# A decoder trunk on one core: VectorE takes the low parts of the attention's weights from GpSimd, and a weight transfer changes shape

## The chip, the cores and the metric

The kernel runs on one NeuronCore of a Trainium2 chip. Its time is the device time of one execution in microseconds (us); 662.78 us is the median of three runs (661.78, 662.78 and 668.63). The engines are named as in the profile: PE (matmul), PEld (its weight loads), DVE (VectorE), ACT (ScalarE), POOL (GpSimd) and SP (SyncE, which issues the transfers).

## The reference

The reference is a two-layer decoder trunk in float32 for 256 tokens of width 1024. The parts that matter here:

```
layer A: h += W_out( B * causal_dwconv3( C * V ) ),  [B|C|V] = rms_norm(h) @ W_in
         h += swiglu(rms_norm(h))                    hidden width 2816
shared:  kv = rms_norm(h) @ w_kv                     six sets: compressed K and V, selected K and V, window K and V
         k_cmp, v_cmp = silu(blocks @ w1) @ w2       blocks of 32 tokens, stride 16, w1 is 2048 x 256 for each
layer B: q, gates from rms_norm(h) @ w_qg
         h += (gate0*o_cmp + gate1*o_slc + gate2*o_win) @ w_o     16 heads of 64, 4 KV groups
         h += swiglu(rms_norm(h))
out = rms_norm(h)
```

## The kernel before

Every product is computed to nearly float32 accuracy from numbers of a shorter format. A weight piece of 128 x 1024 float32 comes in over DMA into a "raw" tile; its **high part** is a rounded copy (`hi`), its **low part** is the difference raw minus high (`lo`). Activations are split in the same way, and three products (high x high, high x low, low x high) stand for one. `split_weights` (lines 302 to 327) does this for a piece: transfer (L316 or L318), high part (L320 on POOL or L322 on ACT), low part (L326), whose columns are divided between POOL and DVE. The last argument, `pool`, says how: False gives all columns to DVE, True all to POOL, "both" half to each, "hi" the high part to POOL, "all" high and low part to POOL. For the pieces of the attention stage it comes from `CFG["units"]`, whose other entry names the ring of buffers ("a" or "r") of the parts. `CFG["eng"]` does the same for single operations: for `q00` (first half of the split of Q0, `q_split`) "ap" means high part on ACT, low part on POOL; "pd" means high part on POOL, low part on DVE.

A piece has a name: K (keys and values for compression, selection and window), Q, V, Y (the compression's first weights w1), GP (gates), O (output projection). A raw tile in the attention stage has four buffers, a part three for each ring.

The order of the work is a text, `CFG["plan"]` (lines 216 to 224), read from left to right: "A" and "r" fetch the next piece of one of two streams (`Stream.ahead`), "K2a" or "Y00" multiply with one, "CB" makes the blocks for the compression (`cmp_blocks`, L768 is the low part of its blocks), "KR" finishes keys (`key_rest`, with `keyf` at L847 and the key copies over DMA at L855), "S" computes the scores of a head, and so on. "|4", "|5" and "|6" say which engines keep this order as written; the others, from "|4" on all of them and from "|5" on all but PE, are ordered by the scheduler when the program is built. Each engine then works through its list in that fixed order.

For Y the matrix w1 lies in memory as 128 rows (row = parity of the token in its block x 64 + channel) of 4096 columns. Piece `Y{st}{q}` takes tokens 4q to 4q+3 of each half of the block, so it needs both halves of the rows' columns and both parities. It is fetched in two transfers of 64 rows (L316), one for each half, each row in two stretches of 512 columns:

```
w1 = a["w1"][st].rearrange("(two d) x -> d two x", two=2)
takes[f"Y{st}{q}"] = [w1[:, :, (4 * half + q) * 512:(4 * half + q + 1) * 512] for half in range(2)], 1024
```

`cmp_piece` (L770) multiplies it with the tokens `lp` of the blocks.

Of the kernel before, what the change touches and what calls it, by code (L numbers as in the profile page):

```python
# [24 lines left out]
DH = 64  # L25
# [98 lines left out]
         'm5': 'p',  # L124
         'm6': 'p',
         'm7': 'd',
         'q00': 'ap',
         'q01': 'ad',
         'q10': 'pd',
         'q11': 'ad',  # L130
         'q20': 'pd',
         'q21': 'ad',
# [36 lines left out]
 'qdma': 0,  # L169
 'sq': {'n1': 0, 'n3': 1},  # L170
 'units': {'GP': ('a', False),
           'K0a': ('a', 'all'),
           'K0b': ('a', False),
           'K1a': ('r', False),
           'K1b': ('r', 'both'),
           'K2a': ('a', 'both'),
           'K2b': ('a', False),
           'K4a': ('a', 'both'),
           'K4b': ('r', 'both'),
           'O0a': ('r', False),  # L180
           'O0b': ('r', 'all'),
           'O1a': ('r', 'all'),
# [10 lines left out]
           'O6b': ('a', 'all'),  # L193
           'O7a': ('a', 'both'),
           'O7b': ('r', True),
           'Q0a': ('a', 'both'),
           'Q0b': ('r', 'both'),
           'Q1a': ('a', False),
           'Q1b': ('r', 'both'),
           'Q2a': ('a', False),  # L200
           'Q2b': ('a', True),
           'Q3a': ('a', True),
           'Q3b': ('a', True),
           'V0': ('a', True),
           'V1': ('r', 'both'),
           'V2': ('r', False),
           'V3': ('a', True),
           'Y00': ('a', True),
           'Y01': ('a', 'both'),
           'Y02': ('r', False),  # L210
           'Y03': ('a', False),
           'Y10': ('r', True),
           'Y11': ('a', True),
           'Y12': ('a', 'both'),
           'Y13': ('r', 'both')}}
CFG["plan"] = """
H4 K2a H7 K0a A H5 A A K0b A K1a H2 A H0 B0 H1 |4 A K1b H3 NR H6 A A A I NS CR0 CR1 A CB0 K2b Q0a K4a CB1 A
Q0b K4b A Y00 A A A Y10 R0 B1 Y11 A V0 A M0 Y01 A Y02 V1 Y03 J0 Y12 A r A KR4 KR2 A |5 Y13 J1 t0 GP Q1a t1 ck
# [9 lines left out]
def trunk(ctx: ExitStack, tc: tile.TileContext, a):  # L228
    nc = tc.nc
# [32 lines left out]
    def bank(name, kind="short", hold=False):  # L262

        b = min((b for b in ring[kind] if b not in held.values()), key=used.get)
        touch(b)
        if hold:
            held[name] = b
        return psum.tile([P, 512], F32, tag=f"b{b}", name=name)
# [7 lines left out]
    def f(ap):  # L276
        return ap.bitcast(F32)
# [24 lines left out]
    def split_weights(src, name, cols, ring, pool):  # L302
        if (name[0], ring) in spare:
            w, hi, lo = spare.pop((name[0], ring))
        else:
            if phase["name"] == "attention" or name[0] == "O" or name[:2] == "kv":
                w = wp.tile([P, 1024], F32, tag="raw", name=f"w_{name}", bufs=4)
            else:
                w = phase["pool"].tile([P, 1024], F32, tag="raw", name=f"w_{name}", bufs=12)
            hi, lo = (wp.tile([P, 1024], F32R, tag=ring + hl, name=f"{hl}_{name}", bufs=3) for hl in "hl")  # L310
            if name[0] == "O":
                spare[name[0], ring] = [x[:, cols:] for x in (w, hi, lo)]
            w, hi, lo = (x[:, :cols] for x in (w, hi, lo))
        if isinstance(src, list):
            for r, part in enumerate(src):
                nc.sync.dma_start(out=w[r * DH:(r + 1) * DH].rearrange("p (two x) -> p two x", two=2), in_=part)  # L316
        else:
            nc.sync.dma_start(out=w, in_=src)  # L318
        if pool in ("hi", "all"):
            nc.gpsimd.tensor_copy(hi, w)  # L320
        else:
            nc.scalar.activation(hi, w, AF.Copy)  # L322
        cut = {False: 0, True: cols, "both": cols // 2, "hi": 0, "all": cols}[pool]
        for eng, c0, c1 in ((nc.gpsimd, 0, cut), (nc.vector, cut, cols)):
            if c0 < c1:
                eng.tensor_tensor(out=lo[:, c0:c1], in0=w[:, c0:c1], in1=f(hi[:, c0:c1]), op=ALU.subtract)  # L326
        return hi, lo

    class Stream:
# [3 lines left out]
        def ahead(self, n=3):  # L333
            while len(self.ready) < n:
                u = next(self.todo, None)
                if not u:
                    return
                self.ready.append(split_weights(u[1], u[0], u[2], u[4] if len(u) > 4 else self.ring, u[3]))
# [22 lines left out]
    takes = {}  # L361
# [5 lines left out]
    for q in range(4):  # L367
        for st in range(2):

            w1 = a["w1"][st].rearrange("(two d) x -> d two x", two=2)  # L370
            takes[f"Y{st}{q}"] = [w1[:, :, (4 * half + q) * 512:(4 * half + q + 1) * 512] for half in range(2)], 1024
        takes[f"V{q}"] = a["w_v"][q], 1024
    takes["GP"] = a["w_g"], KC * 48

# [395 lines left out]
    def cmp_piece(st, q):  # L770
        if q == 0:
            py[st] = bank(f"py{st}", hold=True)
        wh, wl = wa.take()
        for i in range(4):

            lp = 4 * q + 2 * (i % 2) + i // 2
            first, last = q == 0 and i == 0, q == 3 and i == 3
            x = xc[st].rearrange("p hl g (n l) -> p l (hl g) n", l=16)[:, lp]
            nc.tensor.matmul(py[st][:, :256], x, wh[:, i * 256:(i + 1) * 256], start=first, stop=False)
            nc.tensor.matmul(py[st][:, :256], x, wl[:, i * 256:(i + 1) * 256], start=False, stop=last)  # L780
# [316 lines left out]
    def hid(st):  # L1097
# [6 lines left out]
          "Q": lambda x: q_piece(int(x[0]), "ab".index(x[1])), "R": lambda x: q_rest(int(x)),  # L1104
          "P": lambda x: q_split(int(x)), "M": lambda x: cmp_second(int(x)),
          "Y": lambda x: cmp_piece(int(x[0]), int(x[1])), "J": lambda x: cmp_hidden(int(x)),
          "V": lambda x: value_piece(int(x)), "N": lambda x: value_rest(), "GP": lambda x: gate_proj(),
          "GR": lambda x: gate_rest(), "B": lambda x: bias(int(x)), "t": lambda x: hid(int(x)),
# [156 lines left out]
```

## Time and profile before

| | |
|---|---|
| median of 3 runs | 662.78 us |
| profiled execution, its own time | 669.47 us |
| span of the profiled execution | 667.6 us |
| PE busy | 628.9 us (94%) |
| DVE busy | 490.3 us (73%) |
| ACT busy | 379.1 us (57%) |
| POOL busy | 326.0 us (49%) |
| mean granted TensorE clock | 0.976 of full speed |

Shares of busy time are averages over stages: the convolution layer and the first feed-forward layer up to about 300 us, then the projections and the attention up to about 470 us, then the second feed-forward layer. The table says which engine has the most work over all of them, not which one is waited for in the stage that the change touches.

### The profile page before, as it was taken

Reading aid. Unit: us, or ns where it says so; the run is one execution under the profiler, and the core shown is the slowest. Engines: PE = TensorE matmul, PEld = TensorE weight load, DVE = VectorE, ACT = ScalarE, POOL = GpSimd, SP = SyncE. Lnnn points to the kernel's source line nnn. Section 1 sums busy time; section 2 is a strip of 40 time slices with the busy share of each in tenths; the row PEclk is TensorE's granted clock in tenths of the full one; section 3 lists DMA queues with packets and bytes.
Section 4 is the critical chain, followed back from the end, with each engine's and each line's share of the span. In section 5 each row is a group of like instructions: output and inputs, shape, how many; then the busy total and the mean of one; then the engine's idle time right before and its main releaser. Section 6 shows DMA issues by size and latency. Waiting matters only on the chain.

```text
span 667.6 us, 11200 instructions
## 1 busy us (share of the span) xinstructions
PE 628.9 (94%) x4094; PEld 573.1 (86%) x4094; DVE 490.3 (73%) x773; ACT 379.1 (57%) x744; POOL 326.0 (49%) x285
## 2 busy tenths in 40 slices
PE   7999999999999999879959979999899999999995
PEld 7999998899999999769949869889788888888884
DVE  5688777866666666769996998787986666666664
ACT  7544457545555544437655758997766554444543
POOL 3163225754444444547564675757845444444422
PEclk9999999999999999989989889999899999999998
DMA  8978672655555550031767520003975555555001
GB/s 299 356 303 256 214 245 83 220 190 189 189 187 187 183 179 23 1 127 54 194 171 233 166 95 2 17 17 130 407 291 182 186 179 180 187 186 188 1 1 63
DMA packets 37383, 109.52 MB, mean 164 GB/s; under 512 B 5712, under 2 KB 8144, under 8 KB 37328
## 3 DMA queue, kind: packets, MB, share of 16 engines
q1 hardware_dynamic: 37184, 108.55, 48.0%
q8 instruction: 32, 0.52, 0.3%
q10 hardware_dynamic: 144, 0.26, 0.1%
q14 instruction: 23, 0.19, 0.1%
HBM read 107.22 MB, written 1.05 MB: 162 GB/s over the span
## 4 chain that ended last, share of the span: by engine, by line
PE 75%; DVE 14%; issue 3%; POOL 3%; ACT 3%; DMA 1%; SPq 0%; POOLq 0%; DVEq 0%; ACTq 0%
PE pgu L654 22%; PE pgu L656 11%; PE acc L397 4%; PE acc L398 4%; PE acc L396 4%; PE acc L716 3%; PE acc L715 3%; PE acc L714 3%; DVE n L451 2%; PE pcv L398 2%; PE pcv L397 2%; PE pcv L396 2%; DVE xc L768 1%; POOL l_d L326 1%; PE po L1051 1%
## 5 line engine op out<-in xcount | busy, mean ns | idle before, releaser
L654 PE MATMUL pgu<-n,h_gu 128*128 128x512 f32 x704 | 250.6, 398 | 4.1 <-DVE n L451 2.5
L656 PE MATMUL pgu<-n,l_gu 128*128 128x256 f32 x704 | 197.3, 281 | 0.4 <-DVE l_gu L326 0.4
L654 PEld LDWEIGHTS pgu<-n,h_gu 128*128 128x128 f32 x704 | 132.7, 189 | 35.1 <-DVE n L451 2.5
L326 DVE TENSOR_TENSOR l_gu<-w_gu,h_gu 128x1024 fp32r<-128x1024 f32 x88 | 117.1, 1332 | 26.5 <-ACT h_gu L322 25.4
L656 PEld LDWEIGHTS pgu<-n,l_gu 128*128 128x128 f32 x704 | 133.4, 190 | 2.2 <-DVE l_gu L326 1.1
L667 POOL TENSOR_TENSOR gu<-gu,n_rbc 128x512 f32<-128x512 f32 x40 | 53.2, 1332 | 166.0 <-DVE gu L663 145.1
L672 DVE TENSOR_TENSOR av<-sg,gu 128x256 f32<-128x256 f32 x44 | 79.5, 1809 | 67.9 <-ACT sg L670 67.9
L326 POOL TENSOR_TENSOR l_d<-w_d,h_d 128x1024 fp32r<-128x1024 f32 x43 | 105.2, 2450 | 7.7 <-ACT h_d L322 7.2
L322 ACT ACTIVATE h_gu<-w_gu 128x1024 fp32r<-128x1024 f32 x88 | 92.7, 1053 | 7.1 <-PE pb L397 3.5
L418 ACT ACTIVATE a_h<-av 128x256 fp32r<-128x256 f32 x44 | 18.3, 417 | 78.9 <-DVE av L672 78.9
L322 ACT ACTIVATE h_d<-w_d 128x1024 fp32r<-128x1024 f32 x44 | 46.8, 1063 | 24.5 <-PE acc L716 20.4
L396 PE MATMUL acc<-a_h,h_d 128*128 128x256 f32 x176 | 50.6, 289 | 5.1 <-ACT a_h L418 5.1
L670 ACT ACTIVATE sg<-gu 128x256 f32<-128x256 f32 x44 | 18.2, 417 | 62.1 <-POOL gu L667 52.5
L397 PE MATMUL acc<-a_l,h_d 128*128 128x256 f32 x176 | 50.8, 289 | 0.7 <-DVE a_l L421 0.7
L398 PE MATMUL acc<-a_h,l_d 128*128 128x256 f32 x176 | 50.5, 287 | 0.0
L326 DVE TENSOR_TENSOR l_in<-w_in,h_in 128x768 fp32r<-128x768 f32 (+1 forms) x33 | 38.8, 1187 | 10.7 <-ACT h_in L322 9.5
L322 ACT ACTIVATE h_in<-w_in 128x768 fp32r<-128x768 f32 (+1 forms) x33 | 27.1, 824 | 29.7 <-PE pb L397 20.5
L396 PEld LDWEIGHTS acc<-a_h,h_d 128*128 128x128 f32 x176 | 34.3, 196 | 6.4 <-ACT a_h L418 5.6
L661 ACT ACTIVATE gu<-pgu 128x256 f32<-128x256 f32 x88 | 32.4, 370 | 11.4 <-PE pgu L656 11.4
L398 PE MATMUL pcv<-n,l_in 128*128 128x256 f32 x128 | 36.9, 288 | 1.7 <-DVE l_in L326 1.7
L396 PE MATMUL pcv<-n,h_in 128*128 128x256 f32 x128 | 36.7, 287 | 1.5 <-ACT h_in L322 1.5
L663 DVE TENSOR_TENSOR gu<-pgu,gu 128x256 f32<-128x256 f32 x88 | 36.4, 416 | 1.4 <-ACT gu L661 1.3
(432 smaller groups left out, 1642.1 us busy)
## 6 DMA issues: line engine op xcount, KB each, us to landing
w_gu<-in_w_gu SPq DMA_DIRECT2D x88, 512.0 KB, 4.1
w_d<-in_w_down SPq DMA_DIRECT2D x44, 512.0 KB, 3.4
w_in<-in_w_in SPq DMA_DIRECT2D x31, 384.0 KB, 6.4
w_wo<-in_w_out SPq DMA_DIRECT2D x8, 512.0 KB, 6.7
w_kvY<-in_w SPq DMA_DIRECT2D x16, 256.0 KB, 4.2
w_kvV<-in_w_v SPq DMA_DIRECT2D x4, 512.0 KB, 3.7
h<-in_xT SPq DMA_DIRECT2D x3, 256.0 KB, 5.9
out<-y SPq DMA_DIRECT2D x3, 256.0 KB, 2.3
```

The costliest lines, as they stand in the source:

```text
L322: nc.scalar.activation(hi, w, AF.Copy)
L326: eng.tensor_tensor(out=lo[:, c0:c1], in0=w[:, c0:c1], in1=f(hi[:, c0:c1]), op=ALU.subtract)
L396: nc.tensor.matmul(out, wh, xh, start=start, stop=False, skip_group_check=True)
L397: nc.tensor.matmul(out, wh, xl, start=False, stop=False, skip_group_check=True)
L398: nc.tensor.matmul(out, wl, xh, start=False, stop=stop, skip_group_check=True)
L654: nc.tensor.matmul(ps[j][c], uh[:, cols], x[:, :, k], start=k == 0, stop=False, skip_group_check=True)
L656: nc.tensor.matmul(ps[j][c][:, :S], ul[:, cols], x[:, 0, k], start=False, stop=k == KC - 1, skip_group_check=True)
L661: nc.scalar.activation(gus[j][:, c], ps[j][c][:, S:], AF.Copy)
L663: nc.vector.tensor_tensor(out=gus[j][:, c], in0=ps[j][c][:, :S], in1=gus[j][:, c], op=ALU.add)
L667: (nc.gpsimd if j < NF - 2 else nc.vector).tensor_tensor(out=gu, in0=gu, in1=norm.bc.unsqueeze(1).to_broadcast([P, 2, S]), op=ALU.mult)
L672: nc.vector.tensor_tensor(out=av, in0=sg, in1=gu[:, 1], op=ALU.mult)
L714: nc.tensor.matmul(out, xh, wh, start=start, stop=False, skip_group_check=True)
```

## The change

The low parts of all K, Q, V and Y pieces go to DVE whole (entries False), K0a's high part goes from POOL to ACT, and the two splits q00 and q10 take ACT for the high and DVE for the low part. The entries of O stay. A Y piece now holds one parity (q % 2) of eight tokens in each half, so that it can be fetched in one transfer of 128 rows of 1024 columns; `cmp_piece` takes the tokens to match.

```
-         'q00': 'ap',
+         'q00': 'ad',
-         'q10': 'pd',
+         'q10': 'ad',
...
-           'K0a': ('a', 'all'),
+           'K0a': ('a', False),
-           'K1b': ('r', 'both'),
-           'K2a': ('a', 'both'),
+           'K1b': ('r', False),
+           'K2a': ('a', False),
-           'K4a': ('a', 'both'),
-           'K4b': ('r', 'both'),
+           'K4a': ('a', False),
+           'K4b': ('r', False),
-           'Q0a': ('a', 'both'),
-           'Q0b': ('r', 'both'),
+           'Q0a': ('a', False),
+           'Q0b': ('r', False),
-           'Q1b': ('r', 'both'),
+           'Q1b': ('r', False),
-           'Q2b': ('a', True),
-           'Q3a': ('a', True),
-           'Q3b': ('a', True),
-           'V0': ('a', True),
-           'V1': ('r', 'both'),
+           'Q2b': ('a', False),
+           'Q3a': ('a', False),
+           'Q3b': ('a', False),
+           'V0': ('a', False),
+           'V1': ('r', False),
-           'V3': ('a', True),
-           'Y00': ('a', True),
-           'Y01': ('a', 'both'),
+           'V3': ('a', False),
+           'Y00': ('a', False),
+           'Y01': ('a', False),
-           'Y10': ('r', True),
-           'Y11': ('a', True),
-           'Y12': ('a', 'both'),
-           'Y13': ('r', 'both')}}
+           'Y10': ('r', False),
+           'Y11': ('a', False),
+           'Y12': ('a', False),
+           'Y13': ('r', False)}}
...
-        if isinstance(src, list):
-            for r, part in enumerate(src):
-                nc.sync.dma_start(out=w[r * DH:(r + 1) * DH].rearrange("p (two x) -> p two x", two=2), in_=part)
-        else:
-            nc.sync.dma_start(out=w, in_=src)
+        nc.sync.dma_start(out=w, in_=src)
...
-            w1 = a["w1"][st].rearrange("(two d) x -> d two x", two=2)
-            takes[f"Y{st}{q}"] = [w1[:, :, (4 * half + q) * 512:(4 * half + q + 1) * 512] for half in range(2)], 1024
+            w1 = a["w1"][st, q % 2 * DH:(q % 2 + 1) * DH].rearrange("d (half x) -> half d x", half=2)
+            takes[f"Y{st}{q}"] = w1[:, :, q // 2 * 1024:(q // 2 + 1) * 1024], 1024
...
-            lp = 4 * q + 2 * (i % 2) + i // 2
+            lp = 8 * (q // 2) + 2 * i + q % 2
```

## Rows read from the trace of the kernel before

**Rows 1.** The page, chain of waits: shares of the span by engine.
```profile
PE 75%; DVE 14%; issue 3%; POOL 3%; ACT 3%; DMA 1%; SPq 0%; POOLq 0%; DVEq 0%; ACTq 0%
```

**Rows 2.** Windows: length, busy PE, PEld, DVE, ACT, POOL; clock, DMA share, GB/s.
```profile
326.00:336.00 10.00, 9.85 (x74) 9.41 (x72) 9.49 (x9) 8.15 (x12) 6.21 (x3) 1.00 0.55 150
336.00:346.00 10.00, 3.04 (x11) 2.09 (x11) 9.91 (x9) 4.52 (x6) 6.71 (x4) 0.96 0.59 158
346.00:362.00 16.00, 15.65 (x72) 15.04 (x73) 10.25 (x15) 8.10 (x13) 5.91 (x5) 0.81 0.94 252
```

**Rows 3.** Timeline of PE: start, duration, line, tiles, shapes, [idle before, releaser].
```profile
346.35 0.56 PE L779 MATMUL py<-h_kvY,xc 128*128 128x256 f32 x1 [3.88 <-DVE keyf L847]
...
361.12 0.39 PE L780 MATMUL py<-l_kvY,xc 128*128 128x256 f32 x1
...
396.94 0.46 PE L964 MATMUL sa<-kh,q 128*128 128x144 f32 x1 [4.89 <-DVE q L421]
```

**Rows 4.** Timeline of DVE: low parts of the compression's blocks.
```profile
327.52 1.34 DVE L768 TENSOR_TENSOR xc<-cf,xc 64x480 fp32r<-64x480 f32 x2
329.18 8.68 DVE L768 TENSOR_TENSOR xc<-cf,xc 64x480 fp32r<-64x480 f32 x4 [0.33 <-ACT xc L767]
```

**Rows 5.** Timeline of POOL, the same stretch.
```profile
332.20 2.42 POOL L326 TENSOR_TENSOR l_kvY<-w_kvY,h_kvY 128x1024 fp32r<-128x1024 f32 x1 [1.06 <-ACT h_kvY L322]
334.56 2.77 POOL L326 TENSOR_TENSOR l_kvV<-w_kvV,h_kvV 128x1024 fp32r<-128x1024 f32 x1
337.30 2.81 POOL L326 TENSOR_TENSOR l_kvY<-w_kvY,h_kvY 128x1024 fp32r<-128x1024 f32 x1
```

**Rows 6.** Line L326: low parts on DVE, ns min/median/max.
```profile
L326 DVE TENSOR_TENSOR l_gu<-w_gu,h_gu x88: 1209/1224/3458, 92.7 to 644.4; 128x1024 fp32r<-128x1024 f32 x88
```

**Rows 7.** Timeline of DVE, 284 to 395 us.
```profile
284.75 2.05 DVE L672 TENSOR_TENSOR av<-sg,gu 128x256 f32<-128x256 f32 x1 [0.48 <-ACT sg L670]
...
293.14 0.42 DVE L672 TENSOR_TENSOR av<-sg,gu 128x256 f32<-128x256 f32 x1 [0.48 <-ACT sg L670]
...
304.62 0.47 DVE L451 SCALAR_TENSOR_TENSOR n<-h,gains,n 128x256 fp32r<-128x256 f32 x1
...
311.97 2.36 DVE L451 SCALAR_TENSOR_TENSOR n<-h,gains,n 128x256 fp32r<-128x256 f32 x1
...
318.69 1.78 DVE L326 TENSOR_TENSOR l_kvK4a<-w_kvK4a,h_kvK4a 128x512 fp32r<-128x512 f32 x1
...
370.25 0.29 DVE L421 TENSOR_TENSOR hv<-sy,hv 128x128 fp32r<-128x128 f32 x1
370.81 2.38 DVE L421 TENSOR_TENSOR hv<-sy,hv 128x128 fp32r<-128x128 f32 x1 [0.26 <-ACT hv L418]
...
385.81 3.43 DVE L326 TENSOR_TENSOR l_O2b<-w_O2b,h_O2b 128x256 fp32r<-128x256 f32 x1
...
392.57 2.17 DVE L998 TENSOR_TENSOR cb<-cb,cm 128x64 f32<-128x64 f32 x1
```

**Rows 8.** Timeline of ACT: an idle stretch, and a wait for a landing.
```profile
284.30 0.42 ACT L670 ACTIVATE sg<-gu 128x256 f32<-128x256 f32 x1 [3.12 <-DVE gu L667]
...
315.61 1.06 ACT L322 ACTIVATE h_kvK4a<-w_kvK4a 128x1024 fp32r<-128x1024 f32 x1 [3.00 <-DMA w_kvK4a<-in_w_kv]
```

**Rows 9.** Line L316, ns min/median/max; timeline of SP's queue.
```profile
L316 SPq DMA_DIRECT2D w_kvY<-in_w x16: 595/600/630, 318.5 to 346.4; - x16
...
318.51 6.80 SPq L316 DMA_DIRECT2D w_kvY<-in_w  x6
```

**Rows 10.** Transfers: count, KB each, median us from issue to landing.
```profile
w_kvV<-in_w_v SPq DMA_DIRECT2D x4, 512.0 KB, 3.7
...
w<-in_w SPq DMA_DIRECT2D x4, 64.0 KB, 2.4
```

**Rows 11.** Windows as rows 2: one transfer alone, and the fullest stretch.
```profile
282.00:288.00 6.00, 6.00 (x49) 5.81 (x48) 5.00 (x6) 1.58 (x4) 4.44 (x3) 1.00 0.25 87
...
470.00:480.00 10.00, 8.59 (x39) 7.25 (x40) 9.79 (x13) 7.36 (x15) 7.75 (x7) 0.83 1.03 413
```

## The prediction

> **What bounds the kernel now.** I read the page first: the chain of waits lies mostly on PE, then on DVE [rows 1]. The change touches only weights used between the tail of the first feed-forward layer (about 280 us) and the first score heads (about 400 us), so I cut that stretch into windows [rows 2]: PE is full from 326 to 336 and nearly full from 346 to 362, but works 3.04 of 10 us from 336 to 346, and DVE is at 9.91 there. In PE's own order [rows 3] the longest of these waits ends at 346.35 (3.88 us); the last compression product is at 361.12; a further 4.89 us of idleness ends at 396.94, on a DVE split of Q. So PE bounds the stage, except where DVE is late.
>
> **Why DVE is late.** Two low-part subtractions of the blocks (L768) take 1.34 us; the next four, of the same shape, take 8.68 [rows 4]. Beside them POOL runs three low parts end to end [rows 5], and each slow DVE subtraction ends with one of these. So a DVE operation with two operands in SBUF stands still while a POOL low part runs. The same pairs recur [rows 7]: `av` 2.05 against 0.42 us, the norm's low part 2.36 against 0.47, `hv` 2.38 against 0.29, l_O2b 3.43 for 256 columns, a 64-column add 2.17, which at its size would need under 0.3.
>
> **The change, part by part.**
>
> *Low parts to DVE.* Nine full and eleven half units move (K0a, Q2b, Q3a, Q3b, V0, V3, Y00, Y10, Y11 full). A full low part costs DVE 1.23 us unblocked [rows 6], POOL 2.42 [rows 5]; a half adds about 0.6. By place, with the unblocked durations of rows 4 and 7:
> - Tail: `av` gets back 1.6, K0a's low part adds 1.2 but can go into DVE's pauses. K0a's high part goes to ACT, 1.06 us like K4a's, and ACT idles 3.12 us there [rows 8]. I take -1 (0 to -1.6).
> - 310 to 326: the norm's low part gets back 1.9; l_kvK4a and its twin l_kvQ0b, 1.78 at half size, become 1.23 whole, 1.1 together; two more norm low parts of this kind about 1 each: 5.0. K1b, Q0a and K4b add 0.55 each. Net -3.3.
> - 329 to 345: the four subtractions get back 8.68 - 4 x 0.67 = 6.0. Four full low parts (4.9), a half (0.6) and Q0's low part (about 0.7) come in: +0.2. w2s and Q's split, which stand right behind them, were held by the last row of rows 5 and by POOL's own part of the split, about 1 each by my estimate: -1.9. With the line above DVE is 5.2 earlier at 346.35, and PE has 7 us of idleness to give it from.
> - 364 to 374: `hv` 2.1 and the like before it 2.1, against V3 and Q2b 2.5: -1.8, of which PE can use 1.
> - 385 to 397: l_O2b about 2.6, the add 1.9, against Q3a and Q3b 2.5: -2 of PE's 4.89.
>
> Sum -9.2 us (-3 to -13: order kept at the far end, half of it lost at the near one). q00 and q10 are in it. POOL's order is free in this stretch or runs ahead; what comes off it hides nothing. SP issues eight transfers instead of sixteen, 0.60 us each [rows 9]: 4.8 us or more of SP's queue; behind them stand only the key copies, which nothing reads before the scores. I cost that at nothing.
>
> *The transfer.* This is the term that decides. Before, every weight transfer has 64 or 128 as outermost dimension on both sides. The new one has `half d x` on the DRAM side: outermost is 2. No row shows what such a transfer takes. Below: like a V piece, 128 rows of 4 KB, 3.7 us [rows 10]. Above: if a transfer is dealt to the DMA engines along its outermost dimension, it runs on two of the sixteen. One busy engine moves 87/(16 x 0.25) = 21.8 GB/s where a transfer runs alone, and 413/(16 x 1.03) = 25.1 where all are full [rows 11]. Half a piece (262 KB) then takes 12.0 or 10.4 us. The nearest row by size says 3.7; by shape none is near, since no row has an outermost dimension below 64. I take the upper case, and 11.2 us in it, because the instruction offers nothing but two parts to share out.
> The Trainium skill, DMA: Bandwidth & Descriptors, section "Why a DMA increments its semaphore by 16 and not by 1", says it outright: the number of engines is the largest up to 16 that divides the size of the slowest dimension on both sides, here 2; by its "Rules for kernel authors" alone, which prefer one transfer of 128 partitions over two halves, the sum would be -9. No row of this case shows either for such a shape.
>
> All eight pieces would use the same two engines, one after another. First issue 318.51 [rows 9], fixed part 2.4 us by the landing of the 64 KB weights [rows 10]: 320.9. Eight x 11.2 = 89.6, and two V pieces' shares on these engines, 2 x 1.4 (32.8 KB at 23.4 GB/s): 413.3. Four raw buffers keep at least one piece queued. Then ACT 1.06, DVE 1.23 and 1.8 of products (8 at 0.22): 417.4, against 361.5: +56. The wait stands in three queues: SP's next piece waits for a raw buffer, with GP, Q1a and the key copies behind it; ACT's high part waits for the landing, with the high parts of Q0 and the keys behind it; DVE's low part waits for ACT, with `keyf` behind it. PE takes its products in a fixed order and waits for all of them, then for GP, Q1a, V2 and the scores. What hides in it: the relief up to 346 is worth nothing more, since DVE waits anyway; the tail's -1 stays, and so do the later -3. PE comes back from thin work at the lower clock, at most +3; I take +1. Net +53.
>
> **Sum.** The profiled execution took 669.47 (span 667.6), 6.7 above the median of 662.78. 669.5 + 53 = 722.5; put on the median, 716.
>
> **The rivals.**
> - *Two engines* (forecast, 0.70): 716; own range 702 to 727 (10.4 to 12.0 us a piece gives -6 and +6; relief and clock -8 to +5). For: the shape. Against: no row.
> - *Sixteen engines, DVE freed* (0.19): Y pieces land like V, and the -9.2 is all there is: 653.6, range 649 to 659. It decides if a piece holds its engines for less than (361.5 - 4.1 - 320.9 - 2.8)/8 = 4.2 us, and up to 4.2 + 9.2/8 = 5.4 us the change is no slower. For: rows 4, 5, 7 leave little doubt of the blocking.
> - *Sixteen engines, the waits move to DVE's queue* (0.11): a low part that POOL used to wait with now waits on DVE for its landing and its high part, in front of L768, the norm and `keyf`. ACT waited 3.00 us for K4a [rows 8]; two such waits take back 6 of 9: 659, range 655 to 670. For: DVE is at 9.91. Against: half of most units was on DVE already.
>
> **Numbers.** 1% (6.6 us) is about what a measurement of this kernel can tell from no change. Faster 0.18 (nearly all of the second case), same 0.09 (most of the third), slower 0.73. The range 652 to 727 holds most of the first case (about 0.62), the third and most of the second.
>
> **What would show it.** Two engines: Y issues landing after 10 us and more each, growing; ACT's high parts of Y spaced by about 11 us; PE waiting on them; the DMA share near 0.13 (2 of 16) between 330 and 410; the last compression product near 415. If instead Y lands at about 4 us, the first case falls. The blocking: L768 about 0.67 each throughout, `hv` 0.3, `av` 0.42 in the tail. If these stay long, something other than the low parts on POOL holds DVE. Wrong in size: if two engines alone move more than 25 GB/s each, or if the pieces are issued well before 318.

## The result, and the profile after

The changed kernel takes 706.2 us (median of 6 runs, 705.79 to 708.52) against 665.59 us for the kernel before on the same chip (6 runs, 661.78 to 669.49): ratio 1.0617 [1.0562, 1.0671], slower. Its profiled execution has a span of 706.7 us against 667.6; the mean granted clock went from 0.976 to 0.941.

The page's chain of waits, shares of the span by engine, has DMA, which held 1% before, level with DVE in second place [rows 1]:

```profile
PE 63%; DMA 13%; DVE 13%; POOL 4%; ACT 3%; issue 3%; SPq 0%; POOLq 0%; ACTq 0%; DVEq 0%
```

The windows that answer to rows 2 (length, busy PE, PEld, DVE, ACT, POOL; clock, DMA share, GB/s):

```profile
326.00:336.00 10.00, 4.42 (x28) 4.02 (x27) 6.36 (x9) 5.65 (x9) 0.00 (x0) 0.84 0.28 94
336.00:346.00 10.00, 0.00 (x0) 0.00 (x0) 0.00 (x0) 0.00 (x0) 0.00 (x0) 0.50 0.13 51
346.00:362.00 16.00, 5.90 (x15) 3.88 (x16) 7.63 (x9) 5.58 (x7) 0.00 (x0) 0.61 0.23 78
```

From 336 to 346 none of the five engines works at all. The DMA share is 0.13, which is 2 of 16, and those two move 51 GB/s, 25.5 each. ACT's timeline (start, duration, line, tiles, [idle before, releaser]) shows what all wait for:

```profile
325.88 1.06 ACT L318 ACTIVATE h_kvY<-w_kvY 128x1024 fp32r<-128x1024 f32 x1 [9.07 <-DMA w_kvY<-in_w]
346.94 1.06 ACT L318 ACTIVATE h_kvY<-w_kvY 128x1024 fp32r<-128x1024 f32 x1 [15.12 <-DMA w_kvY<-in_w]
...
392.51 1.06 ACT L318 ACTIVATE h_kvY<-w_kvY 128x1024 fp32r<-128x1024 f32 x1 [7.58 <-DMA w_kvY<-in_w]
404.14 1.06 ACT L318 ACTIVATE h_kvY<-w_kvY 128x1024 fp32r<-128x1024 f32 x1 [10.57 <-DMA w_kvY<-in_w]
```

The eight high parts of Y stand over (404.14 - 325.88) / 7 = 11.2 us apart on average. PE follows, and its last compression product ends at 408.4 where it ended at 361.5 before [rows 3], 46.9 us later:

```profile
405.25 0.58 PE L774 MATMUL py<-h_kvY,xc 128*128 128x256 f32 x1 [8.44 <-ACT h_kvY L318]
...
408.01 0.43 PE L775 MATMUL py<-l_kvY,xc 128*128 128x256 f32 x1
```

SP's timeline answers to rows 9, and the page's transfers (KB each, us to landing) to rows 10. The first Y issue is 6 us earlier than before, and a V piece that now shares the queue with Y lands after 19.5 us instead of 3.7:

```profile
312.43 9.23 SPq L314 DMA_DIRECT2D w_kvY<-in_w  x3
321.76 4.06 SPq L314 DMA_DIRECT2D w_kvV<-in_w_v  x1
```

```profile
w_kvV<-in_w_v SPq DMA_DIRECT2D x4, 512.0 KB, 19.5
```

DVE is freed where the change takes a low part off POOL. Its timeline, to be read against rows 4 and 7: eight subtractions of the blocks take 0.68 each and end to end, and the `av` that took 2.05 in the tail takes 0.42. The other `av` there, 0.42 before, now takes 2.32, while `l_d`, a low part that the change leaves on POOL (second fence), runs beside it:

```profile
285.08 0.42 DVE L668 TENSOR_TENSOR av<-sg,gu 128x256 f32<-128x256 f32 x1
...
289.88 2.32 DVE L668 TENSOR_TENSOR av<-sg,gu 128x256 f32<-128x256 f32 x1 [0.48 <-ACT sg L666]
...
328.11 5.44 DVE L764 TENSOR_TENSOR xc<-cf,xc 64x480 fp32r<-64x480 f32 x8
...
419.41 0.28 DVE L417 TENSOR_TENSOR hv<-sy,hv 128x128 fp32r<-128x128 f32 x1
```

```profile
289.54 2.38 POOL L322 TENSOR_TENSOR l_d<-w_d,h_d 128x1024 fp32r<-128x1024 f32 x1 [10.97 <-ACT h_d L318]
```

So the change holds two effects of opposite sign. The experiments take them apart, then size each. Each ratio is to runs of the kernel before on the same chip; its median there was 662.25, 663.48 or 662.97. A ratio is turned into us by multiplying with 663. Single executions of the kernel before lie between 661 and 670, and those of `tail_only` and `middle_only` below fall into two groups some 7 us apart, so terms of a few us are given with their intervals.

### The profile page after: what moved, and what is told of

It reads as the page before. It is cut to its first block, busy times and chain, and to the rows that moved or that the text cites. A ratio compares the mean times of both kernels' runs of the same rounds, so it can differ in the third digit from the quotient of the medians.

```text
span 706.7 us, 11153 instructions
## 1 busy us (share of the span) xinstructions
PE 630.7 (89%) x4094; PEld 571.1 (81%) x4094; DVE 476.3 (67%) x783; ACT 380.1 (54%) x746; POOL 286.6 (41%) x262
## 2 busy tenths in 40 slices
DMA packets 36118, 109.51 MB, mean 155 GB/s; under 512 B 5472, under 2 KB 7904, under 8 KB 36064
## 4 chain that ended last, share of the span: by engine, by line
PE 63%; DMA 13%; DVE 13%; POOL 4%; ACT 3%; issue 3%; SPq 0%; POOLq 0%; ACTq 0%; DVEq 0%
PE pgu L650 19%; DMA w_kvY<-in_w 11%; PE pgu L652 10%; PE acc L393 3%; PE acc L394 3%; PE acc L392 3%; PE acc L711 3%; PE acc L712 3%; PE acc L710 3%; PE pcv L394 2%; PE pcv L393 2%; PE pcv L392 2%; DVE n L447 2%; DVE av L668 2%; DVE p L968 1%
## 5 line engine op out<-in xcount | busy, mean ns | idle before, releaser
L322 DVE TENSOR_TENSOR l_kvY<-w_kvY,h_kvY 128x1024 fp32r<-128x1024 f32 x8 | 9.8, 1225 | 63.2 <-ACT h_kvY L318 63.2
L318 ACT ACTIVATE h_kvY<-w_kvY 128x1024 fp32r<-128x1024 f32 x8 | 8.4, 1056 | 68.6 <-DMA w_kvY<-in_w 68.6
L774 PE MATMUL py<-h_kvY,xc 128*128 128x256 f32 x32 | 13.9, 440 | 34.7 <-ACT h_kvY L318 32.2
L774 PEld LDWEIGHTS py<-h_kvY,xc 128*128 128x128 f32 x32 | 9.9, 313 | 36.7 <-ACT h_kvY L318 34.0
## 6 DMA issues: line engine op xcount, KB each, us to landing
w_kvV<-in_w_v SPq DMA_DIRECT2D x4, 512.0 KB, 19.5
```

## The experiments

**The two halves of the change.** `low_parts_only` has the entries of the change and the transfers of before:

```
 CFG of the kernel after
 for r, part in enumerate(src):        # two transfers of 64 rows, as before
     nc.sync.dma_start(out=w[r * DH:(r + 1) * DH]..., in_=part)
```

> One part alone: the low parts, K0a's high part and the two splits of Q as in the changed kernel, the Y pieces still in two transfers of 64 rows. Theory A (two engines: the outermost dimension of 2 confines each Y transfer to two DMA engines, and only that costs time): Y pieces land after about 4 us, the last compression product ends near 352 us, and the relief of DVE is all that is left: 9 us faster than the kernel before (3 to 13), 652 to 662. Theory B (DVE's queue: low parts that POOL used to wait with stand in DVE's queue and hold up the blocks and keys; the transfer is harmless): as slow as the changed kernel, 40 us slower than before.

Measured: 647.54 us, ratio 0.975 [0.9707, 0.9794]. The low parts alone are worth 16.6 us (13.7 to 19.4), more than the 9 (3 to 13) that were expected.

`transfer_only` has the single transfer with the entries of before:

```
 CFG of the kernel before
+nc.sync.dma_start(out=w, in_=src)     # "half d x": outermost 2 in DRAM
```

> The other part alone: Y pieces in one transfer with outermost dimension 2, low parts and splits divided between POOL and DVE as before. Theory A: 45 to 60 us slower than before, Y high parts on ACT 10 to 12 us apart, and some 5 to 9 us slower than the changed kernel, because POOL's low parts still hold up DVE ahead of the first Y transfer and behind the last. Theory B: within 1% of the kernel before.

Measured: 718.66 us, ratio 1.0818 [1.0758, 1.0878], which is +54 us (50 to 58), and 13 above the changed kernel, where 5 to 9 were expected. Its timelines of SP and of ACT, to be held against those of the changed kernel above:

```profile
317.34 9.44 SPq L314 DMA_DIRECT2D w_kvY<-in_w  x3
326.95 3.96 SPq L314 DMA_DIRECT2D w_kvV<-in_w_v  x1
```

```profile
330.96 1.06 ACT L318 ACTIVATE h_kvY<-w_kvY 128x1024 fp32r<-128x1024 f32 x1 [4.55 <-DMA w_kvY<-in_w]
...
408.48 1.06 ACT L318 ACTIVATE h_kvY<-w_kvY 128x1024 fp32r<-128x1024 f32 x1 [11.27 <-DMA w_kvY<-in_w]
```

From the first high part of Y to the last it takes 77.5 us here and 78.3 us in the changed kernel: DVE's relief leaves the length of the stream as it is. But the stream starts 4.9 us earlier in the changed kernel (312.43 against 317.34), since the work ahead of it is relieved, and this start passes whole into the end: the last compression product ends at 413.4 here and at 408.4 there.

**Is it the outermost dimension?** The bytes, the tile and the single transfer stay; only the layout of `w1` in memory changes. In `one_of_128` a piece is 128 rows of 1024 in a row:

```
-            takes[f"Y{st}{q}"] = w1[:, :, q // 2 * 1024:(q // 2 + 1) * 1024], 1024
+            takes[f"Y{st}{q}"] = a["w1"][st, q], 1024
-        "w1": ... x[n].reshape(16, P, 256).transpose(1, 0, 2).reshape(P, 4096)
+        "w1": ... x[n].reshape(2, 2, 4, 2, DH, 256).transpose(1, 3, 0, 4, 2, 5).reshape(4, P, 1024)
```

> The changed kernel with w1 laid out in DRAM so that a Y piece is 128 rows one after the other: still one transfer of 512 KB, same bytes on the chip, same tokens, outermost dimension 128. Theory A: Y lands after about 4 us, 9 us faster than before (3 to 13), and within 2 us of the kernel with the low parts alone: that eight issues replace sixteen is worth nothing. Theory B: 40 us slower than before, like the changed kernel.

Measured: 646.31 us, ratio 0.9732 [0.9689, 0.9775]. It is the fastest kernel of this study, though not to be told from `low_parts_only` on the same chip (645.25 to 647.28 against 646.51 to 649.06).

`outer_4`, `outer_8` and `outer_16` put one row that nobody reads behind every 32, 16 or 8 rows of this layout, so that the rows no longer merge into one dimension and the outermost is 4, 8 or 16:

```
+            takes[f"Y{st}{q}"] = a["w1"][st, q, :, :n], 1024        # n = 32, 16, 8
+        "w1": ... .reshape(4, k, n, 1024)[:, :, [*range(n), 0]]     # k = 4, 8, 16
```

> As the kernel with 128 rows one after the other, but with an unread row behind every 32 in DRAM, so that the outermost dimension is 4. Theory A: four engines, 5.2 to 6 us per piece (131 KB at 21.8 to 25.1 GB/s), eight of them 45 us from the first issue near 312: last compression product near 364 to 370, so about as long as the kernel before (-1% to +1%), and 10 us longer than with outermost 128. Theory B: 40 us slower than before.

> As the kernel with outermost 4, with an unread row behind every 16 rows in DRAM: outermost dimension 8. If the time of a piece goes with the number of engines, 2.6 to 3.0 us on each of eight; with four the pieces set the pace, with eight they need less than the 4.2 us at which they would: within 4 us of the kernel with outermost 128 (646 to 650). If instead any outermost dimension below 16 costs alike, as slow as with outermost 4, 669.

> As the kernel with outermost 8, with an unread row behind every 8 rows in DRAM: outermost dimension 16. It tells apart why outermost 8 came out 10 us above 128: if the gaps in DRAM cost nothing and only the number of engines counts, as fast as without gaps (645 to 649); if the gaps, or an outermost dimension other than the 128 rows, cost by themselves, near 656.

Measured: `outer_4` 669.06 us, ratio 1.0082 [1.0048, 1.0116]; `outer_8` 656.23 us, ratio 0.9883 [0.9835, 0.993]; `outer_16` 648.67 us, ratio 0.9759 [0.9699, 0.9819]. The gaps themselves cost nothing that shows, since `outer_16` has the most of them; the time falls with every doubling of the outermost dimension. Two sizes were missed: `outer_4` is 23 us above `one_of_128` and not 10, and `outer_8` is 10 above it and not within 4. ACT's high parts of Y, first and last, in `outer_4` and then in `outer_8`:

```profile
321.38 1.06 ACT L318 ACTIVATE h_kvY<-w_kvY 128x1024 fp32r<-128x1024 f32 x1 [6.17 <-DMA w_kvY<-in_w]
...
364.47 1.06 ACT L318 ACTIVATE h_kvY<-w_kvY 128x1024 fp32r<-128x1024 f32 x1 [5.88 <-DMA w_kvY<-in_w]
```

```profile
318.15 1.06 ACT L318 ACTIVATE h_kvY<-w_kvY 128x1024 fp32r<-128x1024 f32 x1 [2.39 <-DMA w_kvY<-in_w]
...
354.19 1.06 ACT L318 ACTIVATE h_kvY<-w_kvY 128x1024 fp32r<-128x1024 f32 x1 [4.65 <-DMA w_kvY<-in_w]
```

They are 6.2 and 5.1 us apart on average, against 11.2 with an outermost dimension of 2 and 3.2 in `one_of_128` (318.06 to 340.7). A stretch of `outer_4` in which DMA moves little but Y runs at a share of 0.27, which is 4.3 of 16:

```profile
322.00:330.00 8.00, 6.69 (x49) 6.49 (x48) 6.36 (x9) 5.16 (x9) 0.00 (x0) 1.00 0.27 105
```

The page's count of packets tells the engines apart once more. In the order of outermost 2 (the changed kernel), 4, 8 and 128:

```profile
DMA packets 36118, 109.51 MB, mean 155 GB/s; under 512 B 5472, under 2 KB 7904, under 8 KB 36064
```

```profile
DMA packets 36134, 109.51 MB, mean 164 GB/s; under 512 B 5488, under 2 KB 7920, under 8 KB 36080
```

```profile
DMA packets 36166, 109.51 MB, mean 167 GB/s; under 512 B 5520, under 2 KB 7952, under 8 KB 36112
```

```profile
DMA packets 36230, 109.52 MB, mean 170 GB/s; under 512 B 5584, under 2 KB 8016, under 8 KB 36176
```

The packets under 512 B grow by 16, 48 and 112, which over the eight Y transfers is 2, 6 and 14 more for each: what it would be if a transfer ended with one small packet for every engine, on 2, 4, 8 and 16 engines. The kernel before, whose Y came in sixteen transfers of 64 rows, counts 5712 on its page, 240 more than the changed kernel: 16 x 16 less 8 x 2. The Trainium skill, DMA: Bandwidth & Descriptors, section "Why a DMA increments its semaphore by 16 and not by 1", says that every engine that takes part closes its share with a write of its own, and that their number is the largest up to 16 that divides the slowest dimension on both sides. The four counts, 5472, 5488, 5520 and 5584, agree with both.

**Is it POOL's subtraction that holds DVE?** `pool_subtracts_too` is `one_of_128`, and POOL repeats the subtractions that the change took from it, into the raw tile that nobody reads any more. DVE keeps all the work; the raw buffer comes free only when POOL is done:

```
+        also = MOVED.get(name[2:])     # the units that POOL had, whole or half
+        if also:
+            nc.gpsimd.tensor_tensor(out=w[:, :n], in0=w[:, :n], in1=f(hi[:, :n]), op=ALU.subtract)
```

> The kernel with 128 rows one after the other (646 us), but behind each low part that DVE took over, POOL does the old POOL part once more, into the raw tile that is dead by then; nobody reads that. Theory A (a POOL subtraction holds up DVE operations with two operands in SBUF): DVE loses again what it gained and still has the added low parts: 662 to 690, L768 and others of 2 us and more beside the POOL subtractions. Rival C (the gain came from low parts that are ready sooner, 1.2 instead of 2.4 us, not from DVE's stalls): 646 to 650, since PE waits for DVE's low parts alone.

Measured: 673.15 us, ratio 1.0131 [1.0084, 1.0179], 4.1% above `one_of_128`. The timelines of DVE and of POOL in it:

```profile
335.32 1.22 DVE L325 TENSOR_TENSOR l_kvV<-w_kvV,h_kvV 128x1024 fp32r<-128x1024 f32 x1
...
337.06 2.82 DVE L325 TENSOR_TENSOR l_kvY<-w_kvY,h_kvY 128x1024 fp32r<-128x1024 f32 x1
339.80 2.56 DVE L423 TENSOR_TENSOR w2s<-w,w2s 128x256 fp32r<-128x256 f32 x1
```

```profile
335.54 3.25 POOL L329 TENSOR_TENSOR w_kvY<-w_kvY,h_kvY 128x1024 f32<-128x1024 f32 x1 [6.01 <-DVE l_kvY L325]
338.76 3.32 POOL L329 TENSOR_TENSOR w_kvV<-w_kvV,h_kvV 128x1024 f32<-128x1024 f32 x1
```

DVE's l_kvY ends at 339.88 and takes 2.82 us where it needs 1.23; POOL's subtraction ends at 338.79. A 256-column w2s, which takes 0.42 in the changed kernel, then stands for 2.56 us beside POOL's next one, which ends at 342.08. The blocking follows POOL's work though no result of it is read. How much of the 4.1% is the blocking and how much the later release of the raw tiles was not separated by a run. PE's longest wait of the stretch from 280 to 420 points to DVE:

```profile
PE py L781 <- DVE l_kvY L325: 7.1, 1, 7.1
```

In `one_of_128` the longest wait of that stretch is 1.6 us, on ACT. What ACT waits for landings in the same stretch grows only from 8.0 us in `one_of_128` to 11.5 in all, and PE itself waits for none.
The Trainium skill, SBUF — State Buffer, section "Who interferes with whom", says that DVE and POOL share a pair of ports, held for a whole instruction by whichever comes first; a DVE operation with two SBUF inputs needs it only against a POOL operation that reads SBUF. The 2.56 us of w2s agree.

**Where the relief lies.** Three kernels each move one stretch of the units and keep the transfers of before:

```
tail_only:    K0a, K2a
middle_only:  K1b K4a K4b Q0a Q0b V0 V1 Y00 Y01 Y10 Y11 Y12 Y13, q00
heads_only:   V3 Q1b Q2b Q3a Q3b, q10
```

> The kernel before with K0a and K2a alone moved to DVE (K0a's high part to ACT), the only low parts that lie beside the tail of the first feed-forward layer. By the prediction's term 1 us faster (0 to 1.6). By the trace of the kernel with the low parts alone, where the first K product starts 6.1 us earlier and the granted clock does not fall there: 4 to 6 us faster, 657 to 659.

> The kernel before with the remaining low parts moved (K1b, K4a, K4b, Q0a, Q0b, V0, V1, all Y, q00), transfers as before. By the prediction's terms for 310 to 345 us: 5.2 faster. With tail alone (5.8 faster) and heads alone (2.7 faster) the parts would add to 14, near the 15 to 16 of all together, if this is 5 to 7 faster (656 to 658).

> The kernel before with V3, Q1b, Q2b, Q3a, Q3b and the high part of q10 moved, the ones beside the first score heads. By the prediction's terms 3 us faster. By the trace of the kernel with the low parts alone, where the stretch from the first score to the first output projection is 9.8 us shorter: 8 to 10 us faster, 652 to 655.

Measured: `tail_only` 657.72 us, ratio 0.9922 [0.9878, 0.9965]; `middle_only` 658.6 us, 0.9912 [0.9873, 0.9951]; `heads_only` 660.76 us, 0.9939 [0.9907, 0.9971]. In us these are -5.2 (2.3 to 8.1), -5.8 (3.2 to 8.4) and -4.0 (1.9 to 6.2), together -15.0 of the -16.6 of all at once. The middle comes out as expected and the tail as its trace said; the heads miss the 8 to 10 us that were read from a trace and lie near the prediction's 3.

The tail in PE's timeline and in a window, both of the kernel before, then both of `tail_only`:

```profile
294.06 0.58 PE L396 MATMUL acc<-a_h,h_d 128*128 128x256 f32 x1 [4.54 <-ACT a_h L418]
```

```profile
296.00:300.00 4.00, 4.00 (x21) 4.00 (x20) 0.99 (x2) 0.91 (x2) 0.00 (x0) 0.50 0.43 135
```

```profile
289.87 0.39 PE L396 MATMUL acc<-a_h,h_d 128*128 128x256 f32 x1 [1.29 <-ACT a_h L418]
```

```profile
296.00:300.00 4.00, 4.00 (x36) 4.00 (x35) 4.00 (x7) 3.73 (x12) 2.94 (x7) 1.00 0.00 0
```

PE's wait falls from 4.54 to 1.29 us. After the long wait the granted clock is 0.50, the lower of the two levels (1.2 GHz), and PE does 21 matmuls in 4 us; without it the clock stays at 1.00 (2.4 GHz) and it does 36. In `pool_subtracts_too`, where POOL subtracts in the tail again, the loss is back: from 292 to 296 PE works 1.80 of 4 us at a clock of 0.73, against 3.31 at 1.00 in `one_of_128`.

The heads, in the window that held PE's second long wait [rows 3], first of before, then of `heads_only`:

```profile
390.00:400.00 10.00, 5.11 (x32) 4.94 (x31) 9.84 (x33) 5.25 (x16) 6.50 (x7) 0.82 0.33 117
```

```profile
390.00:400.00 10.00, 9.78 (x75) 8.75 (x74) 9.81 (x48) 8.90 (x34) 3.41 (x7) 1.00 0.17 55
```

**Does it go on?** `output_too` is `one_of_128` with all low and high parts of the output pieces taken off POOL as well:

```
-           'O0b': ('r', 'all'), 'O1a': ('r', 'all'), ... 'O7b': ('r', True),
+           'O0b': ('r', False), 'O1a': ('r', False), ... 'O7b': ('r', False),
```

> The kernel with 128 rows one after the other, and the low parts and high parts of all output-projection weights taken from POOL too (high on ACT, low on DVE). If POOL's subtractions hold up DVE there as well and DVE is late: 2 to 4 us faster than 646. If DVE and ACT are full beside the score heads (DVE 9.7 of 10 us from 380 to 400), so that 0.7 us more per piece counts: 0 to 4 us slower.

Measured: 652.93 us, ratio 0.9818 [0.9775, 0.986], slower than `one_of_128` (0.9732) by 0.9%, some 6 us, and outside both cases of the expectation. PE's waits (us in total, times, longest), first of `one_of_128`, then of `output_too`:

```profile
PE pgu L649 <- DVE n L446: 2.6, 3, 1.5
```

```profile
PE pgu L649 <- DVE n L446: 6.2, 2, 5.7
```

A wait of 5.7 us on DVE's norm, in front of the second feed-forward layer, is new. DVE's timeline there:

```profile
445.93 0.69 DVE L518 TENSOR_TENSOR h<-acco,h 128x512 f32<-128x512 f32 x1 [3.56 <-PE acco L393]
446.85 2.58 DVE L322 TENSOR_TENSOR l_gu<-w_gu,h_gu 128x1024 fp32r<-128x1024 f32 x1 [0.22 <-ACT h_gu L318]
449.35 1.87 DVE L518 TENSOR_TENSOR h<-acco,h 128x512 f32<-128x512 f32 x3
451.15 1.58 DVE L322 TENSOR_TENSOR l_gu<-w_gu,h_gu 128x1024 fp32r<-128x1024 f32 x1
452.65 3.57 DVE L446 SCALAR_TENSOR_TENSOR n<-h,gains,n 128x256 fp32r<-128x256 f32 x4
```

DVE had its last low part of an output piece done at 433.1 and stood idle for 3.56 us just before. So this wait is not a backlog of the added work: two low parts of the next layer's weights (l_gu) stand ahead of the norm in DVE's list. In `one_of_128` one such low part is done by 442.6, and the next stands behind seven norms. Why the list came out in another order was not tested. The end of the output projection is only 1.8 us later than in `one_of_128` (448.0 against 446.2).

## Why the prediction was right

The time, 706.2 us, lies in the range of the likeliest case (702 to 727) and 10 below its 716. By its steps:

**The transfer: right, and the deciding term.** The forecast read an outermost dimension of 2 as two engines, at 11.2 us a piece, and priced this at +56 with +1 for the clock. Alone, in `transfer_only`, it costs +54. At two engines' 51 GB/s half a piece takes 262 / 25.5 = 10.3 us; with the 2.4 us of fixed part and 2.8 us of V taken off, the 91.7 us from the first issue to the last high part are 10.8 us a piece. ACT's and DVE's queues, which were named, stand still together from 336 to 346, and an issue on SP's takes up to 6.55 us. The Trainium skill, DMA: Bandwidth & Descriptors, section "Rules for kernel authors", does not by itself give the -9 that the prediction reads from it: besides its row on two halves it has one on an outermost dimension below 16, which by its size confines the whole transfer to at most that many engines. The +54 agree with the second.

**The forecast end of the compression, 417.4, came out as 408.4.** The pieces account for 8 x (11.2 - 10.8) = 3.2 us and the first issue at 312.43 instead of 318.51 for 6.1 us, together 9.3 of the 9.0. Of the 6.1 us the relief explains 4.9; `transfer_only`, without it, starts at 317.34.

**The step that failed: the relief under a starved stream.** The prediction let only 4 us of the relief survive, since up to 346 "DVE waits anyway". Between `transfer_only` (1.0818) and the change (1.0617) lie 2.0%, 13 us. DVE does wait from 326 on, but the relief ahead of the first Y issue sets when the stream starts, and that came through whole: 4.9 us between these two. Behind the compression, the heads gave back more than the 3 that were kept: from the first score product to the first output product it takes 35.4 us in the changed kernel (419.5 to 454.9) and 40.4 in `transfer_only` (425.1 to 465.5). These two make 9.9 us; the profiled executions of the two kernels lie 10.8 apart. So the measured +41 (0.0617 x 663) is the +54 less 13, where the prediction took +57 less 4.

**The relief itself: mechanism right, its first term too small.** POOL's subtractions hold DVE, as the prediction said, and `pool_subtracts_too` shows it. One reading of rows 4 and 5 is not exact. The 8.68 us are not four slow subtractions but 2.47, 0.66, 2.75 and 2.70, and the first belongs to a POOL low part that rows 5 leave out:

```profile
L768 DVE TENSOR_TENSOR xc<-cf,xc x8: 642/656/2755, 326.2 to 335.2; 64x480 fp32r<-64x480 f32 x8
```

```profile
328.73 2.40 POOL L326 TENSOR_TENSOR l_kvY<-w_kvY,h_kvY 128x1024 fp32r<-128x1024 f32 x1 [5.29 <-ACT h_kvY L322]
```

The slow three end at 331.65, 335.12 and 337.85, each 0.5 us behind a POOL low part (331.13, 334.62, 337.33), and the fast one (331.68 to 332.34) runs mostly in POOL's pause. This makes the case for the blocking stronger, and the 6.0 us of the sum stay. The -9.2 should have been -16.6. Term by term:

| stretch | predicted | measured alone |
|---|---|---|
| tail | -1 (0 to -1.6) | -5.2 (-2.3 to -8.1) |
| 310 to 345 | -5.2 (its own terms add to -5.0) | -5.8 (-3.2 to -8.4) |
| 364 to 397 | -3 | -4.0 (-1.9 to -6.2) |

The middle and the heads hold. The tail was priced by what DVE gets back on `av`, with K0a alone, and not by what PE loses: a wait of 4.54 us on a_h, and a stretch at half the clock behind it. Nor does `av` gain on balance, since the second one is now held by `l_d`. What is gone is a slow `gu` right ahead of the wait, which in the kernel before stands beside that same `l_d` (POOL, 289.77 to 292.11) and takes 0.69 in `tail_only` and in the changed kernel:

```profile
290.10 2.56 DVE L667 TENSOR_TENSOR gu<-gu,n_rbc 128x512 f32<-128x512 f32 x1
```

How the delay of the first `av` leads to the wait on a_h was not followed step by step. K2a's half, also in `tail_only`, had no part in the prediction's tail.

**Sixteen engines, DVE freed** is what `one_of_128` is: the case was priced at 653.6 us and came out at 646.31, better by the undersized relief. It was the right second case; this change does not reach it. Its break-even, up to 5.4 us a piece, stands between `outer_8` (5.1 us apart, 1.2% faster) and `outer_4` (6.2 us, 0.8% slower), near 5.7 on a straight line between them.

**The waits move to DVE's queue** falls for these units: with all of them on DVE the ratio is 0.975, below the 659 us of that case. A wait in DVE's queue does appear in `output_too`, but behind weights of the next layer, and not by the low parts that were moved.

**SP's saved issues, costed at nothing:** eight issues more in `low_parts_only` than in `one_of_128` make no difference that can be told.

## What to carry to other kernels

Before two transfers are joined into one, read the outermost dimension of both its sides: a transfer of 128 partitions whose DRAM side starts with a 2 ran on two engines and cost 8%, and a new layout of the same bytes in memory took that back. Two engines that share work can slow each other without any wait showing it: look for one shape with two durations (0.66 and 2.5 to 2.8 us), which a merged line or a mean hides, and ask what ran beside the long ones. Price a relieved delay by what the bounding engine waits and by the clock it then runs at, and let a relief ahead of a starved stream count in full, since it moves the stream's start.

## What the runs showed of the hardware that was not expected

**An issue takes longer behind confined transfers.** The line of the Y issues on SP (ns, least, median and most), in the changed kernel, in `outer_4` and in `one_of_128`:

```profile
L314 SPq DMA_DIRECT2D w_kvY<-in_w x8: 512/826/6550, 312.4 to 373.0; - x8
```

```profile
L314 SPq DMA_DIRECT2D w_kvY<-in_w x8: 532/563/673, 311.0 to 347.3; - x8
```

```profile
L314 SPq DMA_DIRECT2D w_kvY<-in_w x8: 327/328/544, 312.3 to 334.7; - x8
```

With two engines an issue of Y takes up to 6.55 us, and the V issue behind three of them 4.06 us, so SP's queue is held as well. What fills up was not tested.

**Eight engines did not give twice the rate of four.** Two engines moved 25.5 GB/s each, and in `outer_4` 105 / (16 x 0.27) = 24.3 GB/s per busy engine. In `outer_8`, in a stretch of Y pieces and other transfers,

```profile
333.00:336.00 3.00, 2.26 (x6) 1.36 (x5) 2.91 (x4) 0.30 (x1) 0.00 (x0) 0.54 0.95 180
```

it is 180 / (16 x 0.95) = 11.8 GB/s. With a share of 0.95 more than Y's eight engines are busy, so the other transfers of the stretch are in it. A low rate at a full share is not peculiar to few engines: `low_parts_only`, with sixteen, moves 225 GB/s at a share of 1.04 from 312 to 320, which is 13.5 each. Why each engine moves so much less stays open. It would account for `outer_8` coming out above what was expected of it; that was not tested.
